# Packed first loads, four norms summed by a matmul with ones, and a last stage cut finer

## The chip, the core and the metric

The kernel runs on one core of a Trainium2 chip. The metric is the device time of one execution in microseconds. The engines have these names in the profile: PE is TensorE (PEld its weight loads), DVE is VectorE, ACT is ScalarE, POOL is GpSimd, and SP is the engine whose queue issues nearly all loads.

## The reference

A trunk of two layers over 256 tokens of width 1024, all in float32. Every layer has an FFN, a token mixer (latent attention in layer 0, forgetting attention in layer 1), a second FFN and a gated embedding. An RMS norm stands ahead of each, and one at the end.

```python
def rms_norm(x, g):
    y = xf * lax.rsqrt(jnp.mean(xf * xf, axis=-1, keepdims=True) + NORM_EPS)
    return (y * g).astype(x.dtype)
...
for i in range(DEPTH):
    h = h + 0.5 * swiglu(rms_norm(h, ffn_norm[i, 0]), ffn_w_in[i, 0], ffn_w_out[i, 0])
    u = rms_norm(h, mix_norm[i])
    h = h + mixer(u)
    h = h + 0.5 * swiglu(rms_norm(h, ffn_norm[i, 1]), ffn_w_in[i, 1], ffn_w_out[i, 1])
    gate = jax.nn.sigmoid(rms_norm(h, ple_norm[i]) @ ple_w_gate[i])
    h = h + gate * (p[i] @ ple_w_proj[i])
return rms_norm(h, final_norm)
```

## The kernel before

**Numbers in two parts.** Weights and activations are split into a high part (rounded to the type float32r) and a low part, the difference. A product is high times high, low times high and high times low. `part` (L225) does it in two matmuls for a weight block of 128x128: the high weights against the activation's high and low part side by side (512 columns, L236), then the low weights against the high part (256 columns, L237). `mm3` (L219) does it in three.

**Weights.** `Weights` (L61) reads them from one plan, in order. SP loads a piece of 128x1024 into one of 4 raw buffers; ACT makes the high part (`high`, L98), DVE the low part (`low`, L102); the pair lies in one of 7 buffers (`PAIRS`). `pump` puts one such conversion into the engines' queues; where it is called in the program fixes the place. Each engine works its queue in the order of the program.

**The FFN** (`ffn`, L322) runs over 22 blocks c. Each has a gate matmul chain `pg` and an up chain `pu`, 16 matmuls each over 8 k-tiles, in banks of PSUM of which the pool `psum` has 7. `evacuate` multiplies a bank by the norm's factor `rb` on DVE (`two`), POOL adds the two halves (`gu`), ACT applies Silu, POOL multiplies (`hid`). The matmuls use the activation times the norm's gain; the factor 1/sqrt(mean + EPS) comes in only at the evacuation. So the first blocks may run before it is known: `waits` holds the banks of block 0 (of blocks 0 and 1 in the very first FFN).

**The norm** (`Norm`, L262). While the stage before ends, ACT squares each k-tile and POOL adds the squares up (`acc`). `by_token` (L300) sums over the partitions with 1-column matmuls (`pst`, L305), DVE adds EPS (L308), and POOL takes the power -0.5 (`rtok`, 128x2, L310). `by_column` (L312) spreads the 256 factors over all partitions by two matmuls with the identity (`pb`, L315) and ACT copies them (`rb`, L318). In the FFN `by_token` stands after the gate chain of block c = 1 and `by_column` after its up chain.

**The embedding** of layer 0 (`ple`, L775) multiplies each of 8 blocks by `rb` (`zg`, L779) and goes on through ACT and DVE to the residual stream. That of layer 1 (`ple_by_token`, L818) has tokens on partitions: for each half of the 128 tokens (t) and each half of the columns a sigmoid, two DVE steps, a square that is summed on ACT, and the product with the final gain; `store` (L840) then forms the mean, the power on POOL, and scales and stores the rows.

**The start.** SP loads pieces of the stream (`state`, with the gains in front) and of the first weights (`slabs`) in turn; ACT and DVE convert k-tile by k-tile; 22 matmuls on zeros (L925) keep TensorE busy until then. `first` (L937) runs four chains at once, two k-tiles for each slab.

Of the kernel before, what the change touches and what calls it, by code (L numbers as in the profile page):

```python
# [19 lines left out]
P = 128  # L20
D = 1024
# [39 lines left out]
class Weights:  # L61
# [20 lines left out]
    def take(self, raws):  # L82

        self.raws.update(enumerate(raws))
        self.fetched = self.ahead = len(raws)
# [56 lines left out]
def trunk(ctx, tc, xT, xt, pT, pos, freq, bf, ffn_first, ffn_in, ffn_out, w_down, w_uq, w_ukv, mla_o,  # L142
# [13 lines left out]
    def plan_ffn(i):  # L156

        plan.extend(ffn_first[k] for k in range(0 if i else KD // 2))
# [41 lines left out]
    mhalf = const.tile([P, 2], F32, name="mhalf")  # L200
# [61 lines left out]
    class Norm:  # L262


        def __init__(self, gain, blocks, dim, tag="u"):
            self.gain, self.dim, self.acc, self.sums = gain, dim, None, None
            self.pair = act.tile([P, blocks, 2, T], F32R, name=tag, bufs=2 if tag == "u" else 1)

        def high(self, b, src, vector=False, cuts=(slice(0, T),)):
            g = g_sb[:, self.gain + b:self.gain + b + 1]  # L270
            for c in cuts:
                if vector:
                    nc.vector.tensor_scalar(self.pair[:, b, 0, c], src[:, c], g, None, op0=ALU.mult)
                else:
                    nc.scalar.activation(self.pair[:, b, 0, c], src[:, c], AF.Copy, scale=g)  # L275

        def low(self, b, src, cuts=(slice(0, T),)):
            g = g_sb[:, self.gain + b:self.gain + b + 1]
            for c in cuts:
                nc.vector.scalar_tensor_tensor(self.pair[:, b, 1, c], src[:, c], g,  # L280
                                               self.pair[:, b, 0, c].bitcast(F32), op0=ALU.mult, op1=ALU.subtract)
# [18 lines left out]
        def by_token(self):  # L300
            pst = self.sums
            if pst is None:
                pst = psm.tile([P, 2], F32, name="pst", tag="small")
                for t in range(2):
                    nc.tensor.matmul(pst[:, t:t + 1], self.acc[:, t * P:(t + 1) * P], ones[:, :1], start=True,  # L305
                                     stop=True)
            v = work.tile([P, 2], F32, name="v")
            nc.vector.tensor_scalar(v, pst, 1.0 / self.dim, EPS, op0=ALU.mult, op1=ALU.add)  # L308
            self.rtok = work.tile([P, 2], F32, name="rtok", bufs=3)
            nc.gpsimd.tensor_tensor(self.rtok, v, mhalf, op=ALU.pow)  # L310

        def by_column(self):  # L312
# [5 lines left out]
            nc.scalar.activation(self.rb, pb, AF.Copy)  # L318
            self.rb2 = self.rb.rearrange("p (o t) -> p o t", o=1).to_broadcast([P, 2, T])


    def ffn(norm, nxt, then=None, first=None, meanwhile=None, later=None):  # L322
# [452 lines left out]
    def ple(pp, norm, nxt):  # L775
# [23 lines left out]
        for c in range(2):  # L799
            w, = W.get()  # L800
            for i in range(4):
                if i % 2 == 0:
                    pe = bank("pe")
                if (c, i) == (1, 3):
                    norm.by_column()
# [4 lines left out]
            if c == 0:  # L810
                norm.by_token()
# [6 lines left out]
    def ple_by_token(pp, norm):  # L818
# [6 lines left out]
        sums = work.tile([P, 2, 3], F32, name="sums", bufs=1)  # L825
# [5 lines left out]
        def gated(t, ps, a, i):  # L831
# [5 lines left out]
            nc.scalar.activation(sg, h[:, t, a], AF.Square, accum_out=sums[:, t, i:i + 1])  # L837
            nc.vector.tensor_mul(es[:, t, a], h[:, t, a], gain[:, a])

        def store(t, n):  # L840
            s = work.tile([P, 1], F32, name="s")
            v = work.tile([P, 1], F32, name="v1")
            r = work.tile([P, 1], F32, name="r")
            nc.vector.reduce_sum(s, sums[:, t, :n], axis=AX.X)
            nc.vector.tensor_scalar(v, s, 1.0 / D, EPS, op0=ALU.mult, op1=ALU.add)
            nc.gpsimd.tensor_tensor(r, v, mhalf[:, :1], op=ALU.pow)
            for i, a in enumerate(half):
                if t and i == 0:
                    nc.scalar.activation(h[:, t, a], es[:, t, a], AF.Copy, scale=r)
                else:  # L850
                    nc.vector.tensor_scalar(h[:, t, a], es[:, t, a], r, None, op0=ALU.mult)
                (nc.scalar if t and i == 0 else nc.sync).dma_start(out[t * P:(t + 1) * P, a], h[:, t, a])
# [35 lines left out]
        for t in range(2):  # L888

            cuts = [half[1]] if t == 0 else [slice(N, N + N // 2), slice(N + N // 2, D)]  # L890
            for i, a in enumerate(cuts):
                last = bank("ps", (P, a.stop - a.start))
                for k in range(KD):
                    b = (k % 2 - 1) * N
                    rows(last, ws[k // 2], norm.pair, k, slice(a.start + b, a.stop + b), t, KD - 1)
                gated(t, last, a, 1 + i)
                if (t, i) == (1, 0):
                    store(0, 2)
        store(1, 3)
# [3 lines left out]
    n0 = Norm(G_FFN, KD, D)  # L903
    slabs = big.tile([P, KD // 2 + 2, D], F32, name="slabs", tag="big")
    tokens = slabs[:, KD // 2:, :]
    W.take([slabs[:, i, :] for i in range(KD // 2)])

    a = 0
    for i, n in enumerate((2, 2, 4, 0)):
        if n:  # L910
            b = GAINS + (2, 4, 8)[i] * T
            nc.sync.dma_start(state[:, a:b], xT[:, a:b])
            a = b
        nc.sync.dma_start(slabs[:, i, :], ffn_first[i])
# [4 lines left out]
    W.fetch()  # L919

# [5 lines left out]
    half = [slice(0, 4 * P), slice(4 * P, 8 * P)]  # L926
    for k in range(KD):
        if k % 2 == 0:
            W.pair()
        n0.high(k, hT[:, k, :])  # L930
        W.high(k // 2, half[k % 2])
        n0.low(k, hT[:, k, :])
        W.low(k // 2, half[k % 2])
# [3 lines left out]
    def first(ps):  # L937
        for k in range(0, KD, 2):
            w, = W.get()
            for j in range(2):  # L940
                for i, p in enumerate(ps):
                    part(p, w, n0.pair, range(k + j, k + j + 1), KD - 1, at=lambda x: (j * 4 + i) * P)
            W.done(w)
            W.pump()
            if k == 0:
# [143 lines left out]
def _layout(x, p, positions, ffn_norm, ffn_w_in, ffn_w_out, mix_norm, mla_w_down, mla_q_norm, mla_w_uq,  # L1089
# [18 lines left out]
    a["ffn_first"] = np.ascontiguousarray(  # L1108
        w[0, :, :, :, :2].transpose(0, 1, 3, 2, 4).reshape(KD // 2, 2, P, 4 * P).transpose(0, 2, 1, 3)).reshape(
            KD // 2, P, D)  # L1110
# [37 lines left out]
_ORDER = ["xT", "xt", "pT", "pos", "freq", "bf", "ffn_first", "ffn_in", "ffn_out", "w_down", "w_uq", "w_ukv", "mla_o",  # L1148
# [22 lines left out]
```

## Time and profile before

| | us |
|---|---|
| median of 3 runs (1001.99 to 1003.73) | 1002.31 |
| profiled execution | 1001.83 |
| its span | 999.9 |
| PE busy | 988.3 |
| DVE busy | 740.9 |
| ACT busy | 517.7 |
| POOL busy | 423.6 |

A row of the timeline has the start and the length in us, then the engine, the line, the operation, and out<-in with shapes; in brackets stands how long the engine was idle before it and what ended that. The lines are those of the kernel before. Matmuls overlap, so from one start to the next is what a matmul costs. The table of stretches has, for each engine, the time busy in the stretch; its last three columns are the granted TensorE clock, the share of the DMA engines and GB/s.

### The profile page before, as it was taken

How to read it: one execution, taken by the hardware profiler on the slowest of the kernel's cores; microseconds unless marked ns; L12 is line 12 of the kernel's file. 1: busy time of each engine (PE TensorE's matmuls, PEld its weight loads, DVE VectorE, ACT ScalarE, POOL GpSimd, SP SyncE). 2: the span in 40 equal slices, each digit the busy share in tenths (PEclk: the TensorE clock that was granted, in tenths of full speed). 3: DMA queues.
4: the chain of work that ended last, by engine and by line, in shares of the span. 5: the costliest groups of instructions: out<-in, count | busy, mean ns of one | idle time of the engine just before them, and what ended most of it. 6: DMA issues, size and time to landing. Idle time of an engine off the chain costs nothing.

```text
span 999.9 us, 16012 instructions
## 1 busy us (share of the span) xinstructions
PE 988.3 (99%) x5940; PEld 874.6 (87%) x5940; DVE 740.9 (74%) x1051; ACT 517.7 (52%) x825; POOL 423.6 (42%) x348
## 2 busy tenths in 40 slices
PE   9999999999999999999999999999999999999996
PEld 7888888998888888889888888899889888888886
DVE  6777879676768787667778876666777778886674
ACT  7555444465655444555555444546445554544552
POOL 0777730110267775111477673211221577671120
PEclk9999999999999999999999999999999999999999
DMA  8566666652356666665366666566443566666561
GB/s 330 176 210 209 190 182 190 186 168 86 102 176 209 189 190 184 193 196 195 127 200 206 190 183 192 182 193 208 148 142 102 188 202 199 189 179 202 178 210 43
DMA packets 51388, 180.54 MB, mean 181 GB/s; under 512 B 5872, under 2 KB 6000, under 8 KB 51312
## 3 DMA queue, kind: packets, MB, share of 16 engines
q1 hardware_dynamic: 50880, 178.75, 57.8%
q8 instruction: 47, 0.77, 0.3%
q10 hardware_dynamic: 432, 0.79, 0.2%
q14 instruction: 29, 0.24, 0.1%
HBM read 178.46 MB, written 1.05 MB: 180 GB/s over the span
## 4 chain that ended last, share of the span: by engine, by line
PE 94%; DVE 3%; ACT 1%; issue 1%; DMA 0%; POOLq 0%; POOL 0%; SPq 0%; ACTq 0%; DVEq 0%
PE pu L236 16%; PE po L236 16%; PE pg L236 16%; PE pu L237 8%; PE po L237 8%; PE pg L237 8%; PE ps L236 5%; PE ps L237 2%; PE ps L223 1%; PE ps L222 1%; PE ps L221 1%; DVE wlo L102 1%; PE pv L221 1%; PE pv L223 1%; PE pv L222 1%; PE po L458 1%
## 5 line engine op out<-in xcount | busy, mean ns | idle before, releaser
L102 DVE TENSOR_TENSOR wlo<-raw,whi 128x1024 fp32r<-128x1024 f32 (+2 forms) x338 | 416.8, 1241 | 14.2 <-ACT whi L98 13.6
L98 ACT ACTIVATE whi<-raw 128x1024 fp32r<-128x1024 f32 (+2 forms) x338 | 336.4, 1027 | 19.8 <-DMA raw<-in_ffn_in_dram 12.1
L331 POOL TENSOR_TENSOR gu<-two 128x256 f32<-128x256 f32 x176 | 235.4, 1338 | 118.0 <-DVE two L329 108.6
L236 PE MATMUL pg<-u,whi 128*128 128x512 f32 x704 | 251.8, 395 | 1.6 <-ACT whi L98 1.1
L236 PE MATMUL pu<-u,whi 128*128 128x512 f32 x704 | 251.2, 395 | 0.0
L236 PE MATMUL po<-hs,whi 128*128 128x512 f32 x704 | 246.3, 394 | 0.0
L237 PE MATMUL pg<-u,wlo 128*128 128x256 f32 x704 | 198.3, 282 | 0.2 <-DVE wlo L102 0.2
L237 PE MATMUL po<-hs,wlo 128*128 128x256 f32 x704 | 198.1, 281 | 0.0
L237 PE MATMUL pu<-u,wlo 128*128 128x256 f32 x704 | 198.1, 281 | 0.0
L236 PEld LDWEIGHTS pg<-u,whi 128*128 128x128 f32 x704 | 132.2, 188 | 32.7 <-ACT whi L98 1.4
L236 PEld LDWEIGHTS po<-hs,whi 128*128 128x128 f32 x704 | 132.2, 188 | 30.4
L236 PEld LDWEIGHTS pu<-u,whi 128*128 128x128 f32 x704 | 132.3, 188 | 30.2
L237 PEld LDWEIGHTS pg<-u,wlo 128*128 128x128 f32 x704 | 132.5, 188 | 0.9 <-DVE wlo L102 0.9
L237 PEld LDWEIGHTS pu<-u,wlo 128*128 128x128 f32 x704 | 132.5, 188 | 0.0
L237 PEld LDWEIGHTS po<-hs,wlo 128*128 128x128 f32 x704 | 132.5, 188 | 0.0
L291 POOL TENSOR_TENSOR acc<-acc,sq 128x256 f32<-128x256 f32 x42 | 46.0, 1095 | 174.1 <-ACT sq L286 173.8
L213 ACT ACTIVATE hs<-hid 128x256 fp32r<-128x256 f32 x88 | 36.8, 418 | 142.4 <-POOL hid L349 140.4
L349 POOL TENSOR_TENSOR hid<-sg,gu 128x256 f32<-128x256 f32 x88 | 105.2, 1195 | 7.0 <-POOL gu L331 0.2
L217 DVE TENSOR_TENSOR hs<-hid,hs 128x256 fp32r<-128x256 f32 x88 | 63.5, 722 | 48.6 <-ACT hs L213 48.6
L329 DVE TENSOR_TENSOR two<-pg,rb 128x512 f32<-128x512 f32 x88 | 60.4, 686 | 47.1 <-PE pg L237 39.1
L275 ACT ACTIVATE u<-state 128x256 fp32r<-128x256 f32 x57 | 29.0, 508 | 125.5 <-DVE state L392 104.7
L343 ACT ACTIVATE sg<-gu 128x256 f32<-128x256 f32 x88 | 36.8, 418 | 78.7 <-POOL gu L331 78.7
(247 smaller groups left out, 1187.6 us busy)
## 6 DMA issues: line engine op xcount, KB each, us to landing
raw<-in_ffn_in_dram SPq DMA_DIRECT2D x172, 512.0 KB, 4.1
raw<-in_ffn_out_dram SPq DMA_DIRECT2D x64, 512.0 KB, 3.6
raw<-in_ffn_out_dram SPq DMA_DIRECT2D x32, 384.0 KB, 3.6
raw<-in_fox_qk_dram SPq DMA_DIRECT2D x16, 512.0 KB, 3.5
raw<-in_mla_o_dram SPq DMA_DIRECT2D x8, 512.0 KB, 4.2
raw<-in_ple_gate_dram SPq DMA_DIRECT2D x8, 512.0 KB, 4.6
raw<-in_fox_o_dram SPq DMA_DIRECT2D x8, 512.0 KB, 3.6
raw<-in_ple_rows_dram SPq DMA_DIRECT2D x8, 512.0 KB, 5.2
```

The lines of the kernel that those rows point to most:

```text
L98: self.nc.scalar.activation(self.pairs[i][0][:, c], self.raws[i][:, c], AF.Copy)
L102: self.nc.vector.tensor_sub(lo[:, c], self.raws[i][:, c], hi[:, c].bitcast(F32))
L213: nc.scalar.activation(hi, src, AF.Copy)
L217: nc.vector.tensor_sub(lo, src, hi.bitcast(F32))
L236: nc.tensor.matmul(ps, hi, x[:, k], start=k == 0, stop=False)
L237: nc.tensor.matmul(ps[:, 1, :], lo, x[:, k, 0, :], start=False, stop=k == last)
L275: nc.scalar.activation(self.pair[:, b, 0, c], src[:, c], AF.Copy, scale=g)
L291: nc.gpsimd.tensor_add(new, self.acc, sq)
L329: nc.vector.tensor_mul(two, ps, norm.rb2)
L331: nc.gpsimd.tensor_add(gu[c, i], two[:, 0, :], two[:, 1, :])
L343: nc.scalar.activation(sg, gu.pop((c, 0)), AF.Silu)
L349: nc.gpsimd.tensor_mul(hid[c], gu.pop((c, 0)), gu.pop((c, 1)))
```

## The change

**First loads.** The stream and the first weights of a k-tile lie in one row of a new tile `lead`: 256 columns of the stream and 512 of weights. K-tile 0 comes with 16 gains in one load, k-tile 1 in one, the others two to a load. The whole `state` is loaded too, later, behind the first four pieces of the plan. For k-tile 0 DVE makes the activation's high part, and `first` runs its four high matmuls ahead of its four low ones.

SP's queue at the start of the program, before:

```order
L912 DMA state<-in_xT_dram 128x592
L914 DMA slabs<-in_ffn_first_dram 128x1024
L912 DMA state<-in_xT_dram 128x512
L914 DMA slabs<-in_ffn_first_dram 128x1024
L912 DMA state<-in_xT_dram 128x1024
L914 DMA slabs<-in_ffn_first_dram 128x1024 x2
L916 DMA raw<-in_ffn_in_dram 128x1024 x2
L918 DMA slabs<-in_xt_dram 128x1024 x2
```

The same place in the changed kernel:

```order
L943 DMA lead<-in_lead_dram 128x784
L944 DMA lead<-in_lead_dram 128x768
L946 DMA lead<-in_lead_dram 128x1536 x3
L948 DMA raw<-in_ffn_in_dram 128x1024 x2
L950 DMA lead<-in_xt_dram 128x1024 x2
L88 DMA raw<-in_ffn_in_dram 128x1024 x2
L952 DMA state<-in_xT_dram 128x2128
```

Seven loads of stream and weights have become five, and the load of the state has moved behind the fourth piece of the plan.

**Four norms.** In the three FFNs that have no `first`, and in the embedding of layer 0, `columns` takes the place of `by_token` and `by_column`: one matmul of a 128x128 matrix of ones with `acc` gives the sum in every partition, DVE adds EPS on 128x256, POOL takes the power on 128x256. In the FFN it stands after block 0; in the embedding where `by_token` stood.

DVE's queue where the second FFN begins, before (`u` is the normed activation, `wlo` low weights, `v` the mean, `two` an evacuation):

```order
L273 TENSOR_SCALAR u<-state 128x256
L280 SCALAR_TENSOR_TENSOR u<-state,u 128x256
L102 TENSOR_TENSOR wlo<-raw,whi 128x1024 x3
L308 TENSOR_SCALAR v<-pst 128x2
L102 TENSOR_TENSOR wlo<-raw,whi 128x1024
L329 TENSOR_TENSOR two<-pg,rb 128x512
L329 TENSOR_TENSOR two<-pu,rb 128x512
```

In the changed kernel (`vb` is the mean of every token in every partition):

```order
L273 TENSOR_SCALAR u<-state 128x256
L280 SCALAR_TENSOR_TENSOR u<-state,u 128x256
L101 TENSOR_TENSOR wlo<-raw,whi 128x1024
L326 TENSOR_SCALAR vb<-pb 128x256
L101 TENSOR_TENSOR wlo<-raw,whi 128x1024 x3
L339 TENSOR_TENSOR two<-pg,rb 128x512
L339 TENSOR_TENSOR two<-pu,rb 128x512
```

The mean stands two weight conversions earlier, and the evacuations still behind the fourth.

**The end.** The last half of the columns of the second 128 tokens is cut into 256, 128 and 128 columns, where it was 256 and 256. All matmuls of the four cuts stand together. The mean is kept as a running sum, one small step for each cut. The last scaling is 384 columns on ACT and 640 on DVE.

DVE's queue at the end of the program, before (`sgr` and `fin` are the gated embedding and the stream by token):

```order
L835 TENSOR_TENSOR sgr<-fin,sgr 128x256
L836 TENSOR_TENSOR fin<-fin,sgr 128x256
L838 TENSOR_TENSOR fin<-fin 128x256
L844 TENSOR_REDUCE s<-sums 128x1
L845 TENSOR_SCALAR v_10692<-s 128x1
L851 TENSOR_SCALAR fin<-fin,r 128x512
```

In the changed kernel:

```order
L846 TENSOR_TENSOR sgr<-fin,sgr 128x128
L847 TENSOR_TENSOR fin<-fin,sgr 128x128
L851 TENSOR_TENSOR fin<-fin 128x256
L856 TENSOR_SCALAR v_10702<-sums,v_10694 128x1
L864 TENSOR_SCALAR fin<-fin,r 128x640
```

The steps behind the last matmul work on 128 columns, and the reduction is gone. The core of the diff:

```diff
+        def columns(self):
+
+            pb = psm.tile([P, T], F32, name="pb", tag="small")
+            nc.tensor.matmul(pb, ones, self.acc, start=True, stop=True)
+            v = work.tile([P, T], F32, name="vb", tag="tmp", bufs=5)
+            nc.vector.tensor_scalar(v, pb, 1.0 / self.dim, EPS, op0=ALU.mult, op1=ALU.add)
+            self.rb = work.tile([P, T], F32, name="rb", bufs=3)
+            nc.gpsimd.tensor_tensor(self.rb, v, mhalf, op=ALU.pow)
...
             blocks(waits[0], norm.pair)
+            norm.columns()
             W.pump(2)
...
             if c == at:
-                norm.by_token()
+                if first:
+                    norm.by_token()
                 W.pump()
...
             if c == at:
-                norm.by_column()
+                if first:
+                    norm.by_column()
...
-                if (c, i) == (1, 3):
-                    norm.by_column()
...
             if c == 0:
-                norm.by_token()
+                norm.columns()
...
+        def mean(t, i):
+
+            v = work.tile([P, 1], F32, name="v1", bufs=4)
+            nc.vector.tensor_scalar(v, sums[:, t, i:i + 1], 1.0 / D, means[t], op0=ALU.mult, op1=ALU.add)
+            means[t] = v
...
+        cuts = [(0, N, D), (1, N, N + T), (1, N + T, N + T + P), (1, N + T + P, D)]
+        lasts = []
+        for i, (t, a, b) in enumerate(cuts):
+            lasts.append(bank("ps", (P, b - a)))
+            for k in range(KD):
+                o = (k % 2 - 1) * N
+                rows(lasts[i], ws[k // 2], norm.pair, k, slice(a + o, b + o), t, KD - 1)
...
+        gated(1, lasts[3], cuts[3][1], 3)
+        weigh(1, slice(N + T, D))
+        mean(1, 3)
+        root(1)
+        c = N - P
+        store(1, [(nc.scalar, slice(0, c)), (nc.vector, slice(c, D))])
...
+    nc.sync.dma_start(lead[:, :2 * KD + ROW], lead0)
+    nc.sync.dma_start(steps[:, 1, :], lead1)
+    for i in range(KD // 2 - 1):
+        nc.sync.dma_start(steps[:, 2 * i + 2:2 * i + 4, :].rearrange("p k n -> p (k n)"), lead2[i])
     for t in range(2):
         nc.sync.dma_start(*W.raw())
     for t in range(2):
         nc.sync.dma_start(tokens[:, t, :], xt[t])
     W.fetch()
+    nc.sync.dma_start(state, xT)
...
+        n0.high(k, steps[:, k, :T], vector=k == 0)
+        nc.scalar.activation(hi[:, c], steps[:, k, T:], AF.Copy)
+        n0.low(k, steps[:, k, :T])
+        rest(hi[:, c], lo[:, c], steps[:, k, T:])
...
+        for i, p in enumerate(ps):
+            nc.tensor.matmul(p, w[1][:, i * P:(i + 1) * P], n0.pair[:, 0], start=True, stop=False)
+        for i, p in enumerate(ps):
+            nc.tensor.matmul(p[:, 1, :], w[2][:, i * P:(i + 1) * P], n0.pair[:, 0, 0, :], start=False, stop=False)
```

More of the change, by code (lines that the diff above doesn't have):

```diff
@@ L80, in raw, with skip @@
         return raw, src
[L82 to L85 removed]
+    def skip(self, n):
+        self.fetched = self.ahead = n
     def fetch(self):
@@ L199, in trunk @@
     nc.gpsimd.memset(ones, 1.0)
-    mhalf = const.tile([P, 2], F32, name="mhalf")
+    mhalf = const.tile([P, T], F32, name="mhalf")
     nc.gpsimd.memset(mhalf, -0.5)
@@ L887, in ple_by_token @@
             gated(t, ps[t], half[0], 0)
[L888 to L898, printed above, removed]
@@ L899, in ple_by_token @@
-        store(1, 3)
-        W.done(*ws)
[L903 to L914, printed above, removed]
+            weigh(t, half[0])
@@ new lines, in ple_by_token @@
+        mean(0, 1)
+        root(0)
+        gated(1, lasts[1], cuts[1][1], 1)
+        store(0, [(nc.vector, a) for a in half])
+        mean(1, 1)
+        gated(1, lasts[2], cuts[2][1], 2)
+        weigh(1, cuts[1][1])
+        mean(1, 2)
+        gated(1, lasts[3], cuts[3][1], 3)
[4 more added lines that the diff above has]
+        store(1, [(nc.scalar, slice(0, c)), (nc.vector, slice(c, D))])
+        W.done(*ws)
+    ROW = T + 4 * P
+    lead = big.tile([P, 2 * KD + KD * ROW + 2 * D], F32, name="lead", tag="big")
@@ L919, in trunk @@
     W.fetch()
+    nc.sync.dma_start(state, xT)
+    n0 = Norm(G_FFN, KD, D, table=lead)
     warm = const.tile([P, T], BF16, name="warm")
```

85 lines of the change are left out of this document (47 added, 38 removed).

## The prediction

> **What bounds the kernel now.** I read the page first, for the engine with the largest share, then the list of what TensorE waited for, then the two ends in the timeline.
>
> ```profile
> span 999.9 us, 16012 instructions
> ...
> PE 988.3 (99%) x5940; PEld 874.6 (87%) x5940; DVE 740.9 (74%) x1051; ACT 517.7 (52%) x825; POOL 423.6 (42%) x348
> ```
> ```profile
> PE pg L236 <- ACT whi L98: 1.1, 1, 1.1
> ...
> PE ps L236 <- DVE os L217: 1.0, 2, 0.7
> ```
>
> TensorE (PE) is busy for 99% of the span, and its longest waits for other engines come to about 1 us each. So time can be won only in three ways: TensorE does less, it starts earlier, or the tail after its last matmul gets shorter. The profiled execution took 1001.83 us (span 999.9 and 1.93 around it); the median of the three runs shown is 1002.31, 0.48 more. I sum against 1001.83 and add 0.48. A measurement of this kernel can tell about 0.2%, 2.0 us, from no change.
>
> **First loads.** The start before, in the timeline:
>
> ```profile
> 5.46 0.63 ACT L98 ACTIVATE whi<-slabs 128x512 fp32r<-128x512 f32 x1 [1.27 <-DMA slabs<-in_ffn_first_dram]
> 5.99 0.49 ACT L275 ACTIVATE u<-state 128x256 fp32r<-128x256 f32 x1
> 6.12 0.69 DVE L102 TENSOR_TENSOR wlo<-slabs,whi 128x512 fp32r<-128x512 f32 x1 [1.41 <-ACT whi L98]
> ...
> 6.14 0.49 PE L236 MATMUL pg<-u,whi 128*128 128x512 f32 x1 [1.14 <-ACT whi L98]
> ...
> 6.72 0.48 DVE L280 SCALAR_TENSOR_TENSOR u<-state,u 128x256 fp32r<-128x256 f32 x1
> ...
> 6.86 0.39 PE L237 MATMUL pg<-u,wlo 128*128 128x256 f32 x1 [0.23 <-DVE wlo L102]
> ...
> 8.20 0.63 ACT L98 ACTIVATE whi<-slabs 128x512 fp32r<-128x512 f32 x1 [0.80 <-DMA slabs<-in_ffn_first_dram]
> ...
> 18.28 0.39 PE L236 MATMUL pg<-u,whi 128*128 128x512 f32 x1
> ```
> ```profile
> 0.00:4.30 4.30, 3.22 (x18) 2.38 (x19) 0.30 (x3) 1.99 (x3) 0.88 (x8) 1.00 0.56 183
> 0.00:6.73 6.73, 4.41 (x23) 2.95 (x23) 1.32 (x5) 3.27 (x6) 0.88 (x8) 1.00 0.70 235
> 0.00:8.93 8.93, 6.47 (x35) 4.81 (x36) 2.86 (x8) 4.67 (x9) 0.88 (x8) 1.00 0.77 264
> ```
>
> The second fence is the table of stretches from the start: its last column, GB/s, times the length is what had been moved by then (0.79, 1.58 and 2.36 MB). Before, ScalarE waits at 5.46 for 0.83 MB (296 KB of gains and stream, 512 KB of weights), and at 8.20 for 1.61 MB. By the table those bytes were through at about 4.4 and 6.8, so a load is usable 1.1 to 1.4 us after its last byte. Now k-tile 0 needs 784 columns, 0.40 MB, through at about 3.3 and usable at 4.2 (a little under one lag, since only one load stands before it). VectorE's high part, which goes there for this k-tile, and its low part, each at the 0.48 of the row at 6.72 or less, give the first matmul at about 5.1 in place of 6.14; the four high matmuls cover the 0.69 of the low weights.
>
> That start is not kept. K-tiles 2 and 3 come in one load whose end is at 1.58 MB, usable at about 7.9, hardly sooner than the 8.20 of before. From there ScalarE's two conversions (0.49 and 0.63 with their overlap), VectorE's 0.69 and six k-tiles of 8 matmuls follow. 32 pairs ran from 6.86 to 18.28, 0.35 each, so a k-tile takes 1.4 us; k-tile 2 cannot end before about 11.0, and the block of c = 2 starts at 11.0 + 5 x 1.4 = 18.0 in place of 18.28. I take -0.4 us, and as bounds -2.0 (no wait after 5.1: 5.1 + 8 x 1.4 = 16.3) and +0.5 (the longer rows land late). The 1.09 MB of the state go behind the four next weight loads and push the fifth back by some 3 us, at the rate between the last two rows of that table (0.78 MB in 2.2 us); weights lead by several blocks there and the blocks have seven banks, so I cost that at nothing, with the +0.5 for the case that the cover is short.
>
> **Four norms.** Where the sum stands in the second FFN, and for the size of the new matmul the one of the MLA stage that has its shape (128x256, f32):
>
> ```profile
> 275.65 0.50 PE L305 MATMUL pst<-ones,acc 128*128 128x1 f32 x4
> 276.01 0.49 PE L236 MATMUL pu<-u,whi 128*128 128x512 f32 x1
> 276.33 0.28 PE L237 MATMUL pu<-u,wlo 128*128 128x256 f32 x1
> 276.45 0.40 PE L236 MATMUL pu<-u,whi 128*128 128x512 f32 x1
> ...
> 278.92 0.60 PE L315 MATMUL pb<-ident,rtok 128*128 128x128 f32 x4
> 279.28 0.48 PE L236 MATMUL pg<-u,whi 128*128 128x512 f32 x1
> ```
> ```profile
> 207.46 0.70 PE L610 MATMUL pk<-turned,twice 128*128 128x256 f32 x2
> 207.80 0.47 PE L221 MATMUL ps<-kv,whi 128*128 128x256 f32 x1
> 208.11 0.28 PE L222 MATMUL ps<-kv,wlo 128*128 128x256 f32 x1
> ```
>
> The old pair of steps holds TensorE from 275.65 to 276.01 and lengthens the pair behind it from 0.35 to 0.44: 0.45 us. The second, from 278.92 to 279.28, does the same: 0.90 together. The one of L610 takes 0.34 and makes the matmul behind it 0.31 where 0.12 is usual: 0.53. So each norm saves 0.37 us of TensorE; in the three FFNs this is on the path, -1.1 us. In the layer-0 embedding VectorE and ScalarE set the pace behind it, and I count nothing.
>
> What replaces ScalarE's copy is a power on POOL over 256 columns. The trace shows that operation only for one and two columns, and an add for 256:
>
> ```profile
> 198.29 0.71 POOL L310 TENSOR_TENSOR rtok<-v,mhalf 128x2 f32<-128x2 f32 x1 [3.90 <-DVE v L308]
> ...
> 276.43 1.62 POOL L310 TENSOR_TENSOR rtok<-v,mhalf 128x2 f32<-128x2 f32 x1 [5.50 <-DVE v L308]
> 280.75 1.44 POOL L331 TENSOR_TENSOR gu<-two 128x256 f32<-128x256 f32 x2 [2.70 <-DVE two L329]
> ...
> 991.64 0.55 POOL L846 TENSOR_TENSOR r<-v,mhalf 128x1 f32<-128x1 f32 x1 [24.18 <-DVE v L845]
> ```
> ```profile
> 276.27 1.23 DVE L102 TENSOR_TENSOR wlo<-raw,whi 128x1024 fp32r<-128x1024 f32 x1
> 279.98 0.69 DVE L329 TENSOR_TENSOR two<-pg,rb 128x512 f32<-128x512 f32 x1 [2.49 <-ACT rb L318]
> ...
> 462.64 0.42 DVE L779 TENSOR_TENSOR zg<-ps,rb 128x256 f32<-128x256 f32 x1 [2.71 <-PE ps L223]
> ```
>
> The 1.62 is 0.71 lengthened: the 1.23 us subtraction on VectorE began just before it, and the power ended 0.55 us after that. Below, the price is half of the row at 280.75, which is two adds of 256 columns: 0.7 us. Above, a straight line through one column (0.55) and two (0.71) gives 0.55 + 255 x 0.16 = 41 us. How much can be hidden? In the FFN the matmul now stands behind the first two blocks, at 272.9 (275.65 less one block, 2.78); with 0.5 for it and 0.4 for VectorE's addition of EPS the power starts near 273.9. VectorE's next evacuations wait for it, and behind those in its queue the low weights of the eighth block; TensorE has seven banks and, by PAIRS, weights for seven blocks, up to 287.4 (279.28 plus three blocks of 2.78, less the 0.37). An evacuation and the weights behind it take 3.3 us, so the result may come at 284: the power may take 10 us. In the embedding the multiply at 462.64 needs it, and the power starts near 457.0: 5.7 us. Up to 5.7 us it costs nothing. I take it as hidden, because two points that lie inside an instruction's start-up say little of its stream, and the add's 256 columns take 0.7 us; but the straight line stays as a rival.
>
> The Trainium skill's "GPSIMD Engine Reference", section 3.1, puts a two-input elementwise operation there at about 2.6 cycles an element, which by its 1.2 GHz would be 0.55 us for 256 columns (an estimate from that page). The add here agrees; no run yet shows that it holds for a power, and against it speaks the same page's 4 cycles for each step of a dependent fp32 chain.
>
> **The end.** TensorE's last cuts, two 256 wide before, and the tail; and, from the chain that ended last, a case of matmuls only 128 wide that each bring their own 4-byte weights:
>
> ```profile
> 986.41 0.28 PE L221 MATMUL ps<-whi,u 128*128 128x256 f32 x1
> ...
> 986.61 0.69 ACT L834 ACTIVATE sgr<-ps,rtok 128x512 f32<-128x512 f32 x1 [1.17 <-PE ps L223]
> ...
> 987.33 0.69 DVE L835 TENSOR_TENSOR sgr<-fin,sgr 128x512 f32<-128x512 f32 x1 [1.93 <-ACT sgr L834]
> ...
> 989.25 0.28 PE L221 MATMUL ps<-whi,u 128*128 128x256 f32 x1
> ...
> 992.37 0.47 ACT L834 ACTIVATE sgr<-ps,rtok 128x256 f32<-128x256 f32 x1 [0.98 <-PE ps L223]
> 993.01 0.42 DVE L835 TENSOR_TENSOR sgr<-fin,sgr 128x256 f32<-128x256 f32 x1
> ...
> 994.47 0.16 DVE L844 TENSOR_REDUCE s<-sums 128x1 f32<-128x3 f32 x1
> ...
> 995.48 0.72 ACT L849 ACTIVATE fin<-fin,r 128x512 f32<-128x512 f32 x1 [1.04 <-POOL r L846]
> ```
> ```profile
> 968.19 1.75 PE ph L870 x16
> ```
>
> A cut of 256 columns is 24 matmuls in 2.84 us, 0.118 each. The change makes two cuts of 128 from the second. If a matmul took time by its columns alone, the two would take 2.84 together. But the 16 transposes, 128 wide, took 1.75 us, 0.109 each, and the four 1-column matmuls of the norm 0.09 to 0.11 each: the weights set a floor. With 0.109 the two cuts take 48 x 0.109 = 5.2 us, so TensorE ends 2.4 us later.
>
> The Trainium skill's "TensorE: Matmul & The Clock Gate", sections "LDWEIGHTS (loading the stationary operand)" and "Weight-path perf modes", has the same floor: columns divided by 1.2 in ns, 107 ns for 128, and a fast load that leaves fp32 out. By it the two cuts would take 5.1 us and the sum be 1002.1, against 999.8 by columns alone. The rows of transposes agree with it; no row here shows a 128-wide matmul of the cuts' own type.
>
> The tail behind the last matmul gets shorter: the sigmoid on 128 columns (0.69 for 512, 0.47 for 256, so about 0.36) saves 0.11; two VectorE steps (0.69 for 512, 0.42 for 256, so about 0.28) save 0.28; VectorE began at 993.01 though the sigmoid ended at 992.84, since the first rows' scaling stood before it, 0.17; the square about what the sigmoid saves, 0.10; the separate reduction with its gap (994.47 to 994.66) 0.19; ScalarE's last scaling on 384 of 512 columns, by the sigmoid's slope, 0.11. Together -0.96. The 512 KB of the last stores stay. The end: +2.4 - 1.0 = +1.4 us; bounds -1.0 and +7 (below).
>
> **Sum:** 1001.83 - 0.4 - 1.1 + 1.4 = 1001.7; with 0.48, **1002.2 us**, no change.
>
> **The rivals.** (a) Forecast: the power is hidden and the narrow cuts pay for their weights. 1002.2, own range 1000.6 (the start at its best) to 1004.2 (the start at its worst and the norms' 1.1 not gained); chance 0.40. (b) The narrow cuts run by their columns, or the first loads land well: without the 2.4 it is 999.8, with the start's bound as well 998.2. For it: 0.118 for 256 columns and 0.39 to 0.28 in the rows' lengths show time by columns; against it the 0.109. Chance 0.24. (c) The power takes 10 to 16 us: at 16 the embedding loses 10.3 and three FFNs 6 each, 1030; chance 0.10. (d) The straight line holds: TensorE runs out of banks and weights in each FFN for 41.4 - 10 = 31.4 us, and the embedding's chain waits 35.7. 1002.2 + 94 + 36 = 1132, slower. It decides from 5.7 us on in the embedding and from 10 us in the FFNs. For it: the only two prices of a power in the trace; against it: both are a start-up. Chance 0.18. (e) 128 columns cost as plain f32 does (the 0.45 for two matmuls of L315, 0.225 each): 48 x 0.225 = 10.8 in place of 2.8, 1002.2 + 5.6 = 1007.8; chance 0.08.
>
> **How the numbers follow.** Faster by over 0.2% is (b), 0.24. Within 0.2% is (a), 0.40. Slower is (c), (d) and (e), 0.36. The range leaves out (d), 0.18, and a little below: 999.0 to 1030.
>
> **What would show it.** First matmul after the warm-up near 5.1 and the block of c = 2 near 18.0. The L324 matmul 0.5 us; rb on POOL under 5.7 us and no TensorE wait for VectorE behind it. If TensorE waits there by tens of microseconds, (d) holds and the forecast is wrong. In the last two cuts matmuls 0.11 us apart; at 0.06 it is (b), at 0.2 it is (e). From the start of the last sigmoid to the end of the span about 6.5 us, where it was 7.5 (999.9 less 992.37).

## The result, and the profile after

The changed kernel takes 1147.26 us (median of 4 runs, 1145.97 to 1148.19), the kernel before beside it 1002.15: a ratio of 1.1442, 95% interval 1.1428 to 1.1456. It is 145 us slower where no change was forecast. The profiled execution took 1145.97 us. Of its page, the busy times, the granted TensorE clock in 40 slices, the shares of the chain that ended last, and one group:

```profile
span 1144.1 us, 16034 instructions
...
PE 1002.9 (88%) x5940; PEld 884.9 (77%) x5940; DVE 737.5 (64%) x1056; ACT 515.5 (45%) x823; POOL 586.6 (51%) x348
...
PEclk9999999999689999995858999999999859999999
...
PE 78%; POOL 15%; DVE 4%; ACT 1%; issue 1%; DMA 1%; SPq 0%; POOLq 0%; ACTq 0%
...
L328 POOL TENSOR_TENSOR rb<-vb,mhalf 128x256 f32<-128x256 f32 x4 | 168.7, 42170 | 11.2 <-DVE vb L326 11.2
```

TensorE runs as many instructions as before, but is not busy for 141 us of the span (1144.1 - 1002.9), where that was 12. POOL, which was on no long path, now holds 15% of the chain, and the four new powers take 42.17 us each. The second FFN in the timeline of after, in order of time:

```profile
274.17 0.59 PE L324 MATMUL pb<-acc,ones 128*128 128x256 f32 x2
...
275.30 42.17 POOL L328 TENSOR_TENSOR rb<-vb,mhalf 128x256 f32<-128x256 f32 x1 [3.10 <-DVE vb L326]
...
317.51 0.69 DVE L339 TENSOR_TENSOR two<-pg,rb 128x512 f32<-128x512 f32 x1 [38.34 <-POOL rb L328]
...
318.35 0.76 PE L235 MATMUL pu<-u,whi 128*128 128x512 f32 x1 [29.63 <-DVE two L339]
320.83 0.58 PE L236 MATMUL pu<-u,wlo 128*128 128x256 f32 x1 [1.73 <-DVE wlo L101]
```

VectorE stands still for 38.34 us in front of its first evacuation. TensorE goes on until its banks are full, then waits 29.63 us for that evacuation, and 1.73 more for low weights that VectorE could not make meanwhile. In the middle of the wait the granted clock, the third column from the end, is at half:

```profile
296.00:300.00 4.00, 0.00 (x0) 0.00 (x0) 0.00 (x0) 0.00 (x0) 4.00 (x1) 0.50 0.00 0
```

In the embedding the first multiply is the one that waits:

```profile
533.87 0.42 DVE L792 TENSOR_TENSOR zg<-ps,rb 128x256 f32<-128x256 f32 x1 [38.33 <-POOL rb L328]
```

How much each part cost is read from how far the same matmul stands later. First rows of the kernel before, then the same ones of the changed kernel; with each its start is what counts.

```profile
289.82 0.40 PE L236 MATMUL pu<-u,whi 128*128 128x512 f32 x1
495.25 0.47 PE L236 MATMUL pg<-u,whi 128*128 128x512 f32 x1
502.69 0.39 PE L236 MATMUL pg<-u,whi 128*128 128x512 f32 x1
788.50 0.47 PE L236 MATMUL pg<-u,whi 128*128 128x512 f32 x1
799.81 0.40 PE L236 MATMUL pg<-u,whi 128*128 128x512 f32 x1
```
```profile
19.60 0.39 PE L235 MATMUL pg<-u,whi 128*128 128x512 f32 x1
280.20 0.40 PE L235 MATMUL pg<-u,whi 128*128 128x512 f32 x1
324.41 0.40 PE L235 MATMUL pu<-u,whi 128*128 128x512 f32 x1
567.56 0.39 PE L235 MATMUL pg<-u,whi 128*128 128x512 f32 x1
611.09 0.42 PE L235 MATMUL pg<-u,whi 128*128 128x512 f32 x1
896.59 0.39 PE L235 MATMUL pg<-u,whi 128*128 128x512 f32 x1
942.07 0.47 PE L235 MATMUL pg<-u,whi 128*128 128x512 f32 x1
1128.73 0.28 PE L220 MATMUL ps<-whi,u 128*128 128x256 f32 x1
```

| place | before | after | later by | what this place adds |
|---|---|---|---|---|
| block c = 2, second matmul | 18.28 | 19.60 | 1.32 | start +1.3 |
| second FFN, behind its norm | 279.28 | 280.20 | 0.92 | norm -0.4 |
| second FFN, behind the wait | 289.82 | 324.41 | 34.59 | +33.7 |
| third FFN, behind its norm | 495.25 | 567.56 | 72.31 | embedding and norm +37.7 |
| third FFN, behind the wait | 502.69 | 611.09 | 108.40 | +36.1 |
| fourth FFN, behind its norm | 788.50 | 896.59 | 108.09 | -0.3 |
| fourth FFN, behind the wait | 799.81 | 942.07 | 142.26 | +34.2 |
| first cut of 256 at the end | 986.41 | 1128.73 | 142.32 | +0.1 |
| end of the span | 999.9 | 1144.1 | 144.2 | end +1.9 |

The three FFNs and the embedding make 141 of the 144 us; the start and the end cost 3.2 together. (18.28, which the prediction names as the start of the block c = 2, is its second matmul; the first began at 17.93. Like is compared with like here.)

### The profile page after: what moved, and what is told of

Read it like the earlier page. It is cut to its first block, busy times and chain, and to the rows that moved or that the text cites. A ratio compares the mean times of both kernels' runs of the same rounds, so it can differ in the third digit from the quotient of the medians.

```text
span 1144.1 us, 16034 instructions
## 1 busy us (share of the span) xinstructions
PE 1002.9 (88%) x5940; PEld 884.9 (77%) x5940; DVE 737.5 (64%) x1056; ACT 515.5 (45%) x823; POOL 586.6 (51%) x348
## 3 DMA queue, kind: packets, MB, share of 16 engines
HBM read 179.52 MB, written 1.05 MB: 158 GB/s over the span
## 4 chain that ended last, share of the span: by engine, by line
PE 78%; POOL 15%; DVE 4%; ACT 1%; issue 1%; DMA 1%; SPq 0%; POOLq 0%; ACTq 0%
POOL rb L328 15%; PE po L235 14%; PE pu L235 13%; PE pg L235 13%; PE po L236 7%; PE pu L236 7%; PE pg L236 7%; PE ps L235 4%; PE ps L236 2%; DVE wlo L101 1%; PE ps L220 1%; PE ps L222 1%; PE ps L221 1%; PE pv L220 1%; PE pv L222 1%
## 5 line engine op out<-in xcount | busy, mean ns | idle before, releaser
L235 PE MATMUL pu<-u,whi 128*128 128x512 f32 x702 | 255.5, 401 | 59.2 <-DVE two L339 59.2
L341 POOL TENSOR_TENSOR gu<-two 128x256 f32<-128x256 f32 x176 | 223.5, 1271 | 107.5 <-DVE two L339 98.2
L235 PEld LDWEIGHTS pu<-u,whi 128*128 128x128 f32 x702 | 134.6, 192 | 90.7 <-issue 59.8
L328 POOL TENSOR_TENSOR rb<-vb,mhalf 128x256 f32<-128x256 f32 x4 | 168.7, 42170 | 11.2 <-DVE vb L326 11.2
L359 POOL TENSOR_TENSOR hid<-sg,gu 128x256 f32<-128x256 f32 x88 | 117.3, 1333 | 6.9
L216 DVE TENSOR_TENSOR hs<-hid,hs 128x256 fp32r<-128x256 f32 x88 | 57.4, 652 | 62.6 <-ACT hs L212 62.6
```

What stands on the lines that cost most here:

```text
L216: nc.vector.tensor_sub(lo, src, hi.bitcast(F32))
L235: nc.tensor.matmul(ps, hi, x[:, k], start=k == 0, stop=False)
L328: nc.gpsimd.tensor_tensor(self.rb, v, mhalf, op=ALU.pow)
L341: nc.gpsimd.tensor_add(gu[c, i], two[:, 0, :], two[:, 1, :])
L359: nc.gpsimd.tensor_mul(hid[c], gu.pop((c, 0)), gu.pop((c, 1)))
```

## The experiments

Theory A: nearly the whole loss is the power's price by the column; the start and the end cost what the table shows, and the sum by ones itself saves TensorE some 0.4 us in an FFN. Its rivals: a price of the wide form that does not go by columns, a slow TensorE clock with a cause of its own, and a sum by ones that saves nothing.

**Old norms in the new kernel.** `columns` goes out again, at all four places:

```diff
-            norm.columns()
...
-                if first:
-                    norm.by_token()
+                norm.by_token()
...
-                if first:
-                    norm.by_column()
+                norm.by_column()
...
+                if (c, i) == (1, 3):
+                    norm.by_column()
...
-                norm.columns()
+                norm.by_token()
```

> The changed kernel with the four norms as they were before (sum by token, power on 128x2, spread by column); the new start and the new end stay. Theory A (the power on 256 columns is the whole loss but some 3 us; the start costs +1.3 and the end +1.9 as read from where the same matmuls stand in the two traces): 1002.15 + 3.2 = 1005.3 us. Rival B (start and end are worth what was forecast, -0.4 and +1.4): 1003.2 us. Rival C (a good part of the loss is TensorE's lower clock from another cause than the waits): over 1010 us, with stretches at a granted clock of 0.5 in the FFNs.

Measured: 1005.08 us, ratio 1.0027 (1.0016 to 1.0038). Theory A. The longest waits of TensorE are short ones again, and the first two of its list belong to the start:

```profile
PE pg L235 <- ACT whi L964: 1.4, 1, 1.4
PE cold L958 <- DVE warm L955: 1.1, 1, 1.1
PE ps L235 <- DVE os L216: 0.9, 2, 0.7
PE pg L235 <- DVE u L280: 0.9, 1, 0.9
```

So 142 us come from the norms, 3 from the start and the end, and the mean granted clock is back at 0.998, where it was 0.937 to 0.939.

**The power on fewer columns.** The rest of the factor gets a constant, so the norm of most tokens is left out:

```diff
-            nc.gpsimd.tensor_tensor(self.rb, v, mhalf, op=ALU.pow)
+            nc.gpsimd.tensor_tensor(self.rb[:, :32], v[:, :32], mhalf[:, :32], op=ALU.pow)
+            nc.gpsimd.tensor_tensor(self.rb[:, 32:], mhalf[:, 32:], mhalf[:, 32:], op=ALU.mult)
```

> The changed kernel with the power on the first 32 columns only; the other 224 of the factor get 0.25 from a multiply, so the norm of those tokens is left out. Theory A (0.163 us for each column and 0.4 for the instruction): power 5.6 us, no wait of TensorE in the FFNs, the embedding just at its limit: 1004 to 1006 us. Rival (the price is one of the wide form, however many columns over two): over 20 us for the power, and over 1050 us in all.

> As the last, with the power on 64 columns. Theory A: power 10.8 us and the factor ready 11.4 after its start; the FFNs lose 0 to 1.5 us each (cover forecast 10 us; by the trace of the changed kernel TensorE stood still 13.4 us after the power began), the embedding 6 to 7: 1010 to 1016 us. Were the cover of the FFNs larger than 12 us, 1010 to 1011; were it below 8, over 1020.

Measured: 1005.3 and 1026.84 us, one run each. The power's rows in the tile's view, for 32 and for 64 columns (shortest, median and longest in ns):

```profile
L328 POOL TENSOR_TENSOR rb<-vb,mhalf x4: 6347/6348/6351, 274.8 to 785.8; 128x32 f32<-128x32 f32 x4
```
```profile
L328 POOL TENSOR_TENSOR rb<-vb,mhalf x4: 11469/11472/11474, 276.6 to 803.5; 128x64 f32<-128x64 f32 x4
```

From 32 to 64 columns the power grows by 5.12 us, from 64 to 256 by 30.70: 0.160 us a column both times, as between the one and two columns of the kernel before (0.55, 0.71). Theory A had 5.6 and 10.8 us, 0.7 too little: besides the columns the wide form has a fixed part of 1.2 us, where one and two columns give 0.4. The price is by the column; the rival with a fixed price is out.

But 64 columns cost 1026.84, over the 1010 to 1016 of theory A. In that run's trace the factor is ready 12.0 us after the power starts (11.47 and 0.50 for the multiply), and TensorE stands later behind the norms of the second, third and fourth FFN by 3.7, 6.1 and 3.6 us. What is hidden, the cover, is thus 8.3, 5.9 and 8.4 us. (The rest of the miss: the embedding lost 8.3 us, not 6 to 7, and the start came 1.2 us later than in the changed kernel.) The cover ends not with the banks but with the low weights of the blocks, which stand in VectorE's queue behind the evacuations. In the second FFN of w64 the waits of TensorE over 1 us are these two:

```profile
291.87 0.39 PE L236 MATMUL pu<-u,wlo 128*128 128x256 f32 x1 [1.66 <-DVE wlo L101]
...
296.01 0.39 PE L236 MATMUL pg<-u,wlo 128*128 128x256 f32 x1 [1.05 <-DVE wlo L101]
```

Nearly the same covers follow from the changed kernel (42.2 less 33.7, 36.1 and 34.2: 8.5, 6.1, 8.0), where the wait is long enough to fill the banks as well.

In the run with 32 columns the embedding lost 2.1 us, more than the factor's delay (it was ready 6.9 us after the power's start, 1.2 beyond the 5.7 that the prediction had found hidden there). TensorE's first matmul of the third FFN, the ones behind it, and two stretches with their clock; then a stretch of the run sqrt (below), where TensorE had waited 2.01 us at the same place:

```profile
486.58 0.80 PE L235 MATMUL pg<-u,whi 128*128 128x512 f32 x1 [2.15 <-DVE u L280]
...
487.39 0.63 PE L235 MATMUL pu<-u,whi 128*128 128x512 f32 x1
...
488.03 0.63 PE L235 MATMUL pu<-u,whi 128*128 128x512 f32 x1
...
486.00:490.00 4.00, 3.42 (x11) 2.94 (x12) 3.73 (x6) 2.60 (x6) 1.57 (x2) 0.57 0.21 83
486.43:489.84 3.41, 3.26 (x10) 2.78 (x11) 3.18 (x6) 2.01 (x4) 1.57 (x2) 0.50 0.12 49
```
```profile
486.00:490.00 4.00, 3.50 (x20) 3.08 (x21) 3.77 (x6) 2.58 (x5) 1.59 (x2) 1.00 0.13 48
```

After a wait of 2.15 us the granted clock was 0.57 over the next 4 us and pairs of matmuls came 0.64 apart in place of 0.35: 1.4 us more, for a wait that was itself under 2.2. (Some 0.4 of it is caught up by 494, where sqrt waits again.)

Why here and not in sqrt? In the clock that the traces record, every change falls on an edge of an even raster of 3.41 us. In w32 the step from 483.02 to 486.43 held 2.00 us without a matmul, and the next one ran at 0.50. In sqrt an edge at 485.10 cut the wait into 0.6 and 1.4 us, and the clock stayed at 1.00. In all profiled kernels, every step with 1.9 us or more without a matmul was followed by half the clock; of the twelve with 1.4 to 1.8 us only three were.

**Another root.** The sum by ones stays at all four places, the root leaves POOL:

```diff
-            nc.gpsimd.tensor_tensor(self.rb, v, mhalf, op=ALU.pow)
+            nc.vector.reciprocal(v, v)
+            nc.scalar.activation(self.rb, v, AF.Sqrt)
```

> The changed kernel with the power replaced by a reciprocal on VectorE and a square root on ScalarE, over the same 256 columns; POOL has no part in the norm. Theory A (the matmul of ones does save 0.4 us of TensorE in each of three FFNs, and only the power's price undid it): 1005.3 - 1.2 = 1004.1 us. Rival (ScalarE's tables are swapped for the root and back, and the conversions of weights behind them come late): at 2 x 1.3 us for each of four norms up to 10 us more, 1005 to 1015 us, with waits of TensorE for weights behind the norm.

Measured: 1006.28 us (5 runs from 1004.8 to 1007.69), ratio 1.0033 (1.0020 to 1.0047). In time that is the rival's. The profiled execution is the one of 1004.80, though, 0.7 above theory A, and the mean granted clock tells the five apart: 0.997 and 0.998 at 1004.80 and 1004.81, 0.996 at 1006.28 and 1006.29, 0.995 at 1007.69. One step of 3.41 us at half the clock takes 0.0017 off the mean and, by the rows above, some 1.5 us; so the median probably has one such step, which the trace does not show.

In the trace the only wait for weights behind an FFN's norm is one of 0.32 us, in the third. The FFNs gained about what theory A says: behind the norms of the second and the fourth, TensorE stands 0.5 and 0.4 us earlier, in the third 0.1. The embedding lost 1.1 (0.45 us behind the kernel before ahead of it, 1.51 at the third FFN). ScalarE's rows there:

```profile
456.92 1.28 ACT L329 ACT_TABLE_LOAD   x1
459.07 0.42 ACT L329 ACTIVATE rb<-vb 128x256 f32<-128x256 f32 x1 [0.88 <-DVE vb L328]
463.32 1.28 ACT L794 ACT_TABLE_LOAD   x1
464.61 0.42 ACT L794 ACTIVATE sg<-zg 128x256 f32<-128x256 f32 x1
```

The table of the sigmoid is loaded again between the first `zg` and its sigmoid, which starts 1.5 us later than in the kernel before (463.10). In the second FFN the second load lies in a pause of ScalarE.

**One part at a time**, each beside tokens: single loads from k-tile 2 on; the last half cut 256 + 256; the sum by ones with the root of sqrt in the three FFNs only; and all three.

```diff
-    for i in range(KD // 2 - 1):
-        nc.sync.dma_start(steps[:, 2 * i + 2:2 * i + 4, :].rearrange("p k n -> p (k n)"), lead2[i])
+    for k in range(2, KD):
+        nc.sync.dma_start(steps[:, k, :], lead2[k // 2 - 1, :, k % 2 * ROW:(k % 2 + 1) * ROW])
...
-        cuts = [(0, N, D), (1, N, N + T), (1, N + T, N + T + P), (1, N + T + P, D)]
+        cuts = [(0, N, D), (1, N, N + T), (1, N + T, D)]
...
```

> The kernel of the run tokens (new start, norms as before, new end) with k-tiles 2 to 7 loaded one to a load instead of two. Theory A (the start loses because TensorE stands still 1.4 us for k-tile 2, whose load ends only with k-tile 3): k-tile 2 usable 1.0 to 1.5 us sooner, no wait of TensorE there, the block of c = 2 1.0 to 1.4 us sooner, 1003.7 to 1004.1 us beside 1005.1 of tokens. Rival (the loads are late because the first 8 us move fewer bytes, whatever their cut): k-tile 2 gets sooner by the bytes of one row only and k-tiles 3 and 4 wait in its place: 1004.6 to 1005.1 us.

> The kernel of tokens with the last half cut 256 + 256 in place of 256 + 128 + 128; all matmuls together and the running mean stay. Theory A (48 matmuls of 128 columns at 0.111 each against 24 of 256 at 0.118): TensorE ends 2.5 us sooner, and the tail gets the forecast 0.5 longer for the wider last cut: 1005.1 - 2.0 = 1003.1 us. Rival (the finer cut pays for itself in the tail, and what the end loses lies in the last stores, which are cut 384 + 640 columns): 1004.5 to 1005.1 us.

> The kernel of tokens with the sum by ones in the three FFNs only, the root taken by a reciprocal on VectorE and a square root on ScalarE; the embedding's norm as before. Theory A (0.4 us of TensorE saved in each FFN; what the run sqrt lost, 1.5 us, lay in the embedding): 1005.1 - 1.2 = 1003.9 us. Rival (the swap of ScalarE's tables costs the FFNs what the matmuls save): 1005.1 us or more.

> The three edits of this call together. Theory A: 1005.1 - 1.2 - 2.0 - 1.2 = 1000.7 us, 1.4 below the kernel before (0.14%). Rival (the starts' landings differ from run to run by as much as the gain): 1001.5 to 1002.5 us, the same as before.

Measured, with the ratio to the kernel before:

| run | us | ratio |
|---|---|---|
| single | 1004.11 | 1.0016 (1.0007 to 1.0025) |
| end256 | 1002.87 | 1.0004 (0.9995 to 1.0013) |
| ffncol | 1003.33 | 1.0008 (0.9999 to 1.0017) |
| all3 | 1001.01 | 0.9986 (0.9977 to 0.9995) |

All four times lie with theory A (1003.7 to 1004.1, 1003.1, 1003.9, 1000.7). For single the trace does not bear out its path. With single loads ScalarE converts k-tile 2 at 7.21, where it was 8.2 to 9.2 in the seven profiled kernels that load it with k-tile 3, TensorE waits only 0.17 us, for that k-tile's low weights, and the block of c = 2 comes 1.6 us sooner than in tokens. But this is lost again, since the norm's factor does not come sooner:

```profile
23.77 0.71 PE L315 MATMUL pb<-ident,rtok 128*128 128x128 f32 x4 [0.75 <-POOL rtok L310]
```

Another 0.42 us go to an evacuation behind it, and at the matmul that stands at 29.91 in the kernel before, single is 1.06 us behind that kernel and tokens 0.96. What single wins over tokens in the traces comes later: 0.5 us at the end of the embedding, where tokens waits longer for an activation, and 0.6 in hundredths over the whole span, whose cause is open. That its time fell where theory A had it is luck. all3 has the same loads and the same kind of wait (0.66), and is 0.7 us behind the kernel before at 29.91.

**The state later.** It is loaded behind two more pieces of the plan, on top of all3:

```diff
-    nc.sync.dma_start(state, xT)
...
             if k == 1:
...
                                         accum_out=n0.sums[:, t:t + 1])
+        nc.sync.dma_start(state, xT)
```

> The kernel all3 with the load of the state (1.09 MB) issued behind two more pieces of the plan. Theory A (in the first FFN the state's bytes keep the next weights away, ScalarE waits 2.65 us for them at 23.94 and spreads the norm's factor late, so that TensorE waits some 0.7 us between 23 and 28): those waits go, 1001.0 - 0.7 = 1000.3 us. Rival (the wait there is set by the norm's own chain, from the squares of the tokens to the power): 1000.9 to 1001.1 us.

Measured: 1002.24 us, ratio 0.9998 (0.9989 to 1.0007). Theory A falls: ScalarE's wait is gone, and TensorE waits longer, 2.06 us where it was 0.66. In all3 first, then in late:

```profile
22.47 0.16 DVE L308 TENSOR_SCALAR v<-sums 128x2 f32<-128x2 f32 x1
25.03 1.23 DVE L101 TENSOR_TENSOR wlo<-raw,whi 128x1024 fp32r<-128x1024 f32 x1 [2.40 <-ACT whi L97]
...
22.79 0.71 POOL L310 TENSOR_TENSOR rtok<-v,mhalf 128x2 f32<-128x2 f32 x1 [21.09 <-DVE v L308]
...
23.55 0.71 PE L315 MATMUL pb<-ident,rtok 128*128 128x128 f32 x4 [0.66 <-POOL rtok L310]
```
```profile
22.98 0.16 DVE L308 TENSOR_SCALAR v<-sums 128x2 f32<-128x2 f32 x1
23.10 1.23 DVE L101 TENSOR_TENSOR wlo<-raw,whi 128x1024 fp32r<-128x1024 f32 x1
...
23.30 1.59 POOL L310 TENSOR_TENSOR rtok<-v,mhalf 128x2 f32<-128x2 f32 x1 [21.60 <-DVE v L308]
...
24.95 0.71 PE L315 MATMUL pb<-ident,rtok 128*128 128x128 f32 x4 [2.06 <-POOL rtok L310]
```

With its weights there in time, VectorE's subtraction begins just ahead of POOL's power, which then takes 1.59 in place of 0.71: the lengthening that the prediction read from 276.43. In best and embed (below), with the same loads, it takes 1.60 and 1.61. That is 0.9 of the 1.4 us; the other 0.5 is that the mean came later. In all3 the late weights had kept VectorE out of POOL's way.

**The last stores as before**, and then **the embedding by ones with its table loaded ahead**:

```diff
-        c = N - P
+        c = N
...
             if c == 0:
-                norm.by_token()
+                norm.columns()
+                table(AF.Sigmoid)
```

> The kernel late with the last scaling and the last stores cut 512 + 512 columns, as the kernel before had them. Theory A (the last store ends 0.3 to 0.4 us later where it holds 640 columns; the scaling on ScalarE takes 0.11 longer): 0.2 to 0.3 us less than late, 1000.0 us. Rival (the two stores run one after the other, by their sum of bytes): as late or 0.1 more.

> The kernel best with the sum by ones in the embedding of layer 0 too, the root on ScalarE and the table of the sigmoid loaded right behind it. Forecast's theory (VectorE and ScalarE set the pace in that stage, and TensorE's 0.4 us there is worth nothing): as best within 0.3 us. Rival (TensorE sets it): 0.4 us less. A second rival (ScalarE's two table loads, 1.3 us each, hold back the embedding's conversions): 0.5 to 1.5 us more.

Measured: best 1001.62, ratio 0.9996 (0.9988 to 1.0005); embed 1004.04, ratio 1.0016 (1.0007 to 1.0025). From the last scaling to the end of the span it is 4.42 in best and 4.47 in all3, so the cut of the stores is worth 0.1 at most. What separates the medians of best and late seems to be the clock: five of late's eleven executions, with a mean clock of 0.996 and 0.997, took 1002.60 to 1003.44, the others 1000.99 to 1002.24; of best's twelve only three took over 1002, at 0.994 to 0.997. embed is 2.4 us worse than best, more than any of its theories: TensorE waits 2.07 for the third FFN's first activation, and the clock falls behind that wait as in the run w32 (0.60 over 486 to 490). Nine of its eleven executions have a mean clock of 0.997 or less; the other two took 1001.80 and 1002.18. So some 1.5 of the 2.4 seems to be the clock, and the rest lies in the range of the second rival: with both table loads ahead of the conversions, VectorE waits 1.87 us for ScalarE's at 461.65, and the first `zg` comes 1.3 us later than in the kernel before.

**The norms alone.** The kernel before, with only the edit of ffncol:

> The kernel before with one change: the sum by ones in the three FFNs without the first, the root by a reciprocal on VectorE and a square root on ScalarE. Start, embedding and end are those of before. Theory A (each norm saves TensorE 0.4 to 0.6 us, and that is on the path): 1002.2 - 1.5 = 1000.7 us, faster by 0.15%. Rival (what ffncol won over tokens hung on the new start or end): 1002.0 to 1002.4 us.

Measured: 1001.07 us, ratio 0.9988 (0.9979 to 0.9997): theory A's way with a little less than its 1.5: 1.2 us faster than the kernel before (the interval just leaves out no change), and as fast as all3 with its new start and end. The trace has 0.5 us in the second FFN, 0.1 in the third, where TensorE then waits 0.33 for low weights, and 0.5 in the fourth.

## Why the prediction was wrong, by its steps

- **The power (the step that failed).** The prediction took the price near the lower bound, the add's 0.7 us, "because two points that lie inside an instruction's start-up say little of its stream". They said nearly all of it: 0.16 a column, 41 us by that line, 42.17 measured. An add is another operation, and its price said nothing of a power's. The estimate from the Trainium skill's "GPSIMD Engine Reference", section 3.1 (0.55 us), was near the add (0.74 for one of 256 columns) and failed by a factor of 77 for the power. The rival (d), 1132 us at a chance of 0.18, was what happened; the measured 1147 lies 15 above it, since the three FFNs cost some 10 more, with less of the power hidden, and the embedding, the start and the end 2, 1.7 and 0.5.
- **What of the power is hidden.** 10 us were forecast for the FFNs (its 287.4 should be 287.2 by its own terms, which changes nothing); w64 shows 8.3, 5.9 and 8.4. The path was the right one (low weights behind the evacuations), and up to the first wait its length fits too: in the second FFN of w64 that wait is 1.66, so 10.3 of 12.0 us were hidden. Not counted was that the low weights of the next blocks come late as well, behind the other evacuations that had been held up (waits of 1.05 and 0.23). In the third FFN the first wait is 4.43 already. In the embedding 35.7 lost were forecast, and 37.7 show with the third norm's saving in it.
- **The sum by ones.** Forecast 0.37 saved in each FFN and nothing in the embedding. Shown: 0.4 behind the second FFN's norm in the changed kernel, 1.2 us for the three in normsonly (0.5, 0.1 and 0.5), no gain left in the embedding.
- **First loads.** -0.4 forecast, with +0.5 as the worse bound; +1.3 measured. The first real matmul came at 5.61 (5.1 forecast, 6.14 before). The step that failed is the load of k-tiles 2 and 3, "usable at about 7.9":

```profile
9.16 0.51 ACT L275 ACTIVATE u<-lead 128x256 fp32r<-128x256 f32 x1 [2.99 <-DMA lead<-in_lead_dram]
9.58 0.61 ACT L965 ACTIVATE whi<-lead 128x512 fp32r<-128x512 f32 x1
...
10.34 0.47 PE L235 MATMUL pg<-u,whi 128*128 128x512 f32 x1 [1.08 <-DVE u L280]
...
0.00:7.00 7.00, 5.92 (x25) 4.36 (x26) 2.84 (x7) 3.14 (x5) 1.09 (x8) 1.00 0.66 212
```

  It was usable at 9.16, and both conversions came behind it, where before the stream's had been made ahead. By 7.0 us 1.48 MB had been moved in place of 1.67 (212 and 239 GB/s). But bytes are not all of it: end256 and ffncol, with the same queue, moved 253 GB/s in that time, and the load was usable only at 8.21 and 8.70, some 1.8 and 2.2 us after its 1.58 MB were through by the table (at 6.45), where the forecast took a lag of 1.1 to 1.4. Why stays open. The pairing costs 1.6 us at the block of c = 2 (tokens against single), but by 29.91 that is no longer seen, since the norm's factor sets the time there.
- **The state's load, costed at nothing.** In the changed kernel that is what it cost: TensorE stands 1.32 us behind the kernel before at 18.28 and 1.33 at 29.91. In all3, where TensorE is there sooner, ScalarE waits 2.65 us for a late weight; the run late shows that this hid a clash of VectorE and POOL, so that moving the load won nothing.
- **The end.** +1.4 forecast, +1.9 measured. The 48 narrow matmuls run from 1131.58 to 1136.78, 0.111 each (0.109 forecast), so the two cuts take 5.3 us where the one of 256 took 2.8:

```profile
1131.58 0.23 PE L220 MATMUL ps<-whi,u 128*128 128x128 f32 x1
...
1136.78 0.28 PE L222 MATMUL ps<-wlo,u 128*128 128x128 f32 x1
...
1137.15 0.37 ACT L845 ACTIVATE sgr<-ps,rtok 128x128 f32<-128x128 f32 x1 [1.23 <-PE ps L222]
...
1139.52 0.62 ACT L862 ACTIVATE fin<-fin,r 128x384 f32<-128x384 f32 x1 [0.91 <-POOL r L869]
```

  The steps of the tail shortened by 0.74 (2.37 from the sigmoid to the scaling, 3.11 before), close to the forecast. From there to the end it took 4.58 in place of 4.42, where 0.11 less was forecast: this is the term that was missed, and the tail won 0.6 in all, not 1.0. end256 confirms the size: without the narrow cuts 2.2 us come back.

## What to carry to other kernels

Where a change widens an operation that has been seen only on a few elements, fit a line through those few and take it seriously: two short cases of the same operation say more than a wide case of another one. Count what hides a wait to the first thing that starves, here converted weights and not banks, and count the blocks behind it too. Time won ahead of a step is kept only if what that step waits for comes sooner as well: single won 1.6 us at the start and lost it at the first norm. A step that is cheap for TensorE can move its cost to an engine that was on no path: the sum by ones leaves the same 256 values in every partition, and a root taken there works on 256 columns where two were enough.

## What the runs showed of the hardware

- POOL's power costs 0.160 us for each column (128 partitions at once) from 32 to 256 columns and 1.2 besides, 42.17 us for 256; its add of 256 takes 0.74. VectorE's reciprocal on 128x256 takes 1.75, where its multiply takes 0.42.
- TensorE's clock is at 0.5 in the long waits, and for a step of 3.41 us after a wait of 2.1 us too (w32, embed), though not after every one (sqrt, 2.01 us): what counts is how much of the wait falls into one step. The Trainium skill's "TensorE: Matmul & The Clock Gate", Part 1, puts the fall after an idle window of about 3.4 us; the length of the steps here agrees, but 2.0 us without a matmul within one was enough. After the waits of 30 us the low clock cost nothing to be seen: the losses with 64 and with 256 columns differ by 30.0, 30.0 and 30.6 us, the ready times by 30.2. In the second and fourth FFN of w64 the clock did not fall, and TensorE waited there for low weights instead.
- A power of two columns on POOL takes 0.71 us alone and 1.59 to 1.61 where a subtraction of 128x1024 on VectorE (1.23) began 0.2 us ahead of it (late, best, embed).
- Loads at the start differ between kernels with the same queue by up to 1 us: k-tile 2 was usable at 8.21 in one and at 9.16 in another.
